# One-instruction modulation sums, bias and scale by section, the sums spread over merges, output projection and feed-forward, and other feed-forward pieces, in a two-layer DiT block on one core

## The chip, the cores and the metric

One core of a Trainium2 chip runs the whole kernel in one launch. The metric is device time in microseconds (us); lower is better. The times of before are three runs, and one more execution was profiled.

## What is computed

Two layers of a hybrid block on 512 latent tokens `x` and 256 context tokens `ctx`, width 1024, in float32. Cut to what matters here:

```python
def adaln(cond, w_mod, b_mod):
    return jnp.split(jax.nn.silu(cond) @ w_mod + b_mod, N_MOD, axis=-1)
...
        sh1, sc1, gt1, sh2, sc2, gt2 = [m[:, None, :] for m in adaln(c, w_mod[l], b_mod[l])]
        csh1, csc1, cgt1, csh2, csc2, cgt2 = adaln(c_ctx, w_mod[l], b_mod[l])
        h = modulate(rms_norm(x, norm1[l]), sh1, sc1)
        a_b, a_c, a_x, q, k, v, u, sv, g = project(h, w_in[l], q_gain[l], k_gain[l])
...
        x = x + gt1 * merge_branches(...)
        x = x + gt2 * swiglu(modulate(rms_norm(x, norm2[l]), sh2, sc2), w_ff1[l], w_ff3[l], w_ff2[l])
```

The context tokens go through the same weights with their own modulation `c_ctx`; in the second layer only their keys and values are needed. `merge_branches` is `(g_a * y_a + g_b * y_b + g_c * y_c) @ w_o`, with three sigmoid gates, each a projection of 1024 columns.

Each layer has six modulation vectors ("sections" 0 to 5: shift, scale and gate of the first half, shift, scale and gate of the second), each a product of a 1024-vector with a 1024x1024 matrix.

## The kernel before, in words

Activations lie transposed: channels in the 128 partitions, 8 blocks of them, tokens along the row (0 to 511 latent, 512 to 767 context). Every float32 operand of a large product is split in a high and a low part; a product is three matmuls, high x high, high x low, low x high (`mm`, L233 to L241, the matmuls at L240). Weights come by `load_piece` (L219 to L227): SP issues the load into `ws` (five buffers), ACT casts to `wh`, POOL or DVE subtracts to get `wl` (both by `split`, L229 to L231). All loads, of weights and of the modulation matrices, stand in one queue, SP's, which issues in order.

The stages of a layer: first norm (`norm`, `norm_stats` L349 to L372: squares on ACT, added to `nacc` by DVE at L358, a column sum on PE at L361 into `pst`, `ms` at L363, its power on POOL, `RR` at L368, transposed to `pRB`; then `norm_apply` L374 to L386 writes `ny` and the split arena tiles `A`), projections, attention, then the merges (L809 to L851). A merge j computes three gates of 768 columns: PE into banks, ACT's tanh at L815 into a `gate` buffer (two for the gates a and c of a width), DVE multiplies the branch into it at L821 and adds the parts at L830 and L836; ACT and POOL split the result `z`. The output projection (`wo_j`, L860 to L875) and the second norm by halves (`norm_half`) follow. In layer 0 the feed-forward takes pairs of columns by seven products in place of eight (`pair_product`, L310 to L346; `ff_pair`, L936 to L978; a pair has two of them, for `w_ff1` and `w_ff3`); the first pair is computed plainly (`first_pair`). The results `u`, split again by `keep_u`, go into `ff2_j` (L993 to L1007), piece by piece: layer 0's 22 column blocks come in the pieces of L980, and after each piece the second matrix of those blocks is added to X, eight outputs j. In the last piece `lagged` (L423 to L437) does outputs 0 to 3 in full, then 4 to 7 for the x columns, then 4 to 7 for the context columns, with the next layer's norm of x between them.

The modulation is done on DVE, from rows: one 128-row block of the transposed matrix is multiplied with the condition, which lies in all partitions (`sbc`), and summed along the row. `mod_block` (L152 to L171) does a block of a section: two loads of 128x512 (`wm`, six buffers, L156), and for each condition two multiply-and-sum instructions (L162, each followed by a read of the accumulator), one that adds both halves and the bias (L165) and in three sections a scaling (L169 or L171). The blocks of the first norm are called where it is. The other 80 come from a generator, `bg_all`: 32 blocks of layer 0 with two conditions, 16 of layer 1 with two, 32 of layer 1 with one, which makes 128 pairs of block and condition; `pump` draws from it after merges, output-projection columns, and feed-forward steps. `bg_stage` (L175 to L179) can hold a block's load back: POOL copies one column of a tile into the new `wm` buffer (L178), so that the load waits for that tile. Before, that tile is the last branch b from the merges to the end of the output projection and none later.

The program is written in one order, but the Tile framework schedules it with a model of the engines: what stands in which queue is decided there, by what an instruction waits for and not only by where it was written.

Of the kernel before, what the change touches and what calls it, by code (L numbers as in the profile page):

```python
# [9 lines left out]
F32 = mybir.dt.float32  # L10
# [21 lines left out]
NX = 6  # L32
# [5 lines left out]
def dit_block(ctx: ExitStack, tc: tile.TileContext, xT, conds, vecs, ident_in, rope_c, rope_s,  # L38
# [57 lines left out]
    def f(t):  # L96
        return t.bitcast(F32)
# [54 lines left out]
    def mod_block(l, sec, b, cs, stage):  # L152
        parts = []
        for hh in range(2):
            t = stage()
            nc.sync.dma_start(t, w_modT[l, sec * KD + b][:, hh * 512:(hh + 1) * 512])  # L156
            parts.append(t)
        for c in cs:
            acc = sm.tile([P, 2], F32, tag="macc", name="macc", bufs=4)
            for hh in range(2):  # L160
                junk = wp.tile([P, 512], F32, tag="junk", name="junk", bufs=1)
                nc.vector.scalar_tensor_tensor(junk, parts[hh], 1.0, sbc[:, c, hh * 512:(hh + 1) * 512],  # L162
                                               op0=ALU.mult, op1=ALU.mult, accum_out=acc[:, hh:hh + 1])
            m = MOD[l][:, sec, b, c:c + 1]
            nc.vector.scalar_tensor_tensor(m, acc[:, 0:1], vcol(l, V_BM + sec * KD + b), acc[:, 1:2],  # L165
                                           op0=ALU.add, op1=ALU.add)
            if sec in (1, 4):
                g, v = (G1, V_N1) if sec == 1 else (G2, V_N2)
                nc.vector.tensor_scalar(g[l][:, b, c:c + 1], m, 1.0, vcol(l, v + b), op0=ALU.add, op1=ALU.mult)  # L169
            elif sec == 2:  # L170
                nc.vector.tensor_scalar(GT1[l][:, b, c:c + 1], m, 0.5, None, op0=ALU.mult)  # L171

    gate_mods = [None]

# [6 lines left out]
    def wm_stage():  # L181
        return wp.tile([P, 512], F32, tag="wm", name="wm", bufs=6)

    def bg_all():
        for sec in (2, 4, 3, 5):
            for b in range(KD):
                mod_block(0, sec, b, (0, 1), bg_stage)
                yield
        for sec in (1, 0):
            for b in range(KD):  # L190
                mod_block(1, sec, b, (0, 1), bg_stage)
                yield
        for sec in (2, 4, 3, 5):
            for b in range(KD):
                mod_block(1, sec, b, (0,), bg_stage)
                yield
# [269 lines left out]
    n_stage = [0]  # L466

    def first_stage():

        t = wm_stage()  # L470
        n_stage[0] += 1
        if n_stage[0] <= 6:
            nc.gpsimd.tensor_copy(t[:, 0:1], X[NX][:, 0:1])
        return t

    for l in range(2):
# [79 lines left out]
        if l == 0:  # L556
            six = [wide[0][:, 0:512], wide[0][:, 512:], wide[1][:, 0:512], wide[1][:, 512:], pst("D"), pst("D")]
            RB = norm_stats(X, *XS)
            for k in range(KD):
                for sec in (1, 0):  # L560
                    mod_block(0, sec, k, (0,), first_stage)
# [147 lines left out]
        if l == 0:  # L709
            def ctx_mods():  # L710
                for k in range(KD):
                    for sec in (1, 0):
                        mod_block(0, sec, k, (1,), wm_stage)
                    yield
# [118 lines left out]
        def merge_b(j, tag):  # L833
# [6 lines left out]
            if not last:  # L840
                pump(3)
# [18 lines left out]
        def wo_j(j, sg):  # L860
# [14 lines left out]
            pump()  # L875
# [6 lines left out]

        gate_mods[0] = None


        def plain(f0, f1, U):
            for n in range(f0, f1):
# [14 lines left out]
                pump()  # L902

        def keep_u(su, U):
            hi, lo = two("u", W)
            split(su, hi, lo)
            U.append((hi, lo))

        def first_pair(U):
# [15 lines left out]
            for n in range(2):  # L925
# [8 lines left out]
                keep_u(su[n], U)  # L934

        def ff_pair(m, U):  # L936
# [142 lines left out]
```

## Time and profile before

| | |
|---|---|
| median of three runs | 1995.39 us (1991.87 to 1998.12) |
| the profiled execution | 1999.56 us, its span 1997.8 us |
| granted TensorE clock | 0.979 |
| PE busy | 1888.2 us (95%), 10150 matmuls |
| DVE busy | 1252.6 us (63%) |
| ACT, POOL busy | 746.9 us (37%), 836.1 us (42%) |
| modulation loads | 224 of 256 KB, 4.1 us each from issue to landing |

PE is TensorE, DVE VectorE, ACT ScalarE, POOL GpSimd, SP the engine that issues loads. A row of a group gives line, engine, operation, tiles (out<-in, without buffer numbers), shapes, count, busy us and mean ns, and after a second bar the idle time before them and what ended it. A row of waits reads "engine line <- what it waited for: us in all, times, longest". A row of a time line gives start, length, engine and line, and in brackets an idle time just before. Where DVE_READ_ACCUMULATOR stands, it belongs to the instruction ahead of it.

### The profile page before, as it was taken

What the parts mean: (1) busy time and instruction counts of PE and PEld (TensorE: products, weight loads), DVE (VectorE), ACT (ScalarE), POOL (GpSimd) and SP (SyncE); (2) the same over time, 40 slices, a digit from 0 to 9 for tenths busy, and PEclk for the clock granted to TensorE, in tenths of its full rate; (3) what the DMA queues carried; (4) which work ended last, traced back from release to release, by engine and by line L of the source; (5) the groups of instructions that cost most, each with busy time, mean ns of one, the idle gap of its engine ahead of it and who ended that gap; (6) DMA issues with size and microseconds to landing.
All of it is one profiled execution on the core that took longest, in us unless ns stands there. A gap on an engine that the chain in (4) does not pass through costs nothing.

```text
span 1997.8 us, 28465 instructions
## 1 busy us (share of the span) xinstructions
PE 1888.2 (95%) x10150; PEld 1661.1 (83%) x10150; DVE 1252.6 (63%) x2454; ACT 746.9 (37%) x1459; POOL 836.1 (42%) x720
## 2 busy tenths in 40 slices
PE   5789999989799899999999997999999999999999
PEld 4578998878679799999999996787888888888887
DVE  7987776999999974655667556648633362322322
ACT  4346766212112642423232235447533353313121
POOL 5577744645432332415142236754333243413231
PEclk9899999999989999999999998999999999999999
DMA  8833211644569222212122214410233244332311
GB/s 288 275 116 99 67 32 30 209 164 143 190 218 337 88 70 63 85 48 80 59 75 68 64 62 143 157 43 6 80 103 93 97 145 144 100 101 90 109 38 65
DMA packets 123871, 221.96 MB, mean 111 GB/s; under 512 B 14160, under 2 KB 22096, under 8 KB 123728
## 3 DMA queue, kind: packets, MB, share of 16 engines
q1 hardware_dynamic: 121664, 216.99, 33.5%
q10 hardware_dynamic: 2064, 3.15, 0.5%
q8 instruction: 80, 1.31, 0.3%
q14 instruction: 63, 0.52, 0.1%
HBM read 212.22 MB, written 5.24 MB: 109 GB/s over the span
## 4 chain that ended last, share of the span: by engine, by line
PE 59%; DVE 4%; issue 2%; ACT 1%; POOL 1%; DMA 0%; ACTq 0%; DVEq 0%; POOLq 0%; SPq 0%
PE wide L240 22%; PE pD L240 18%; PE wide L317 7%; PE pD L317 7%; PE pF L240 1%; PE pO L777 1%; PE pPT L771 1%; PE wide L745 1%; DVE ptl L774 0%; DVE nm L749 0%; DVE nacc L358 0%; DVE xr L998 0%; POOL wl L231 0%; DVE qq L549 0%; DVE qb L537 0%
## 5 line engine op out<-in xcount | busy, mean ns | idle before, releaser
L231 POOL TENSOR_TENSOR wl<-ws,wh 128x512 fp32r<-128x512 f32 (+2 forms) x338 | 458.8, 1368 | 550.1 <-ACT wh L230 392.2
L240 PE MATMUL wide<-A,wh 128*128 128x512 f32 (+2 forms) x1728 | 479.3, 373 | 43.6 <-ACT gate L815 19.0
L240 PEld LDWEIGHTS wide<-A,wh 128*128 128x128 f32 x1728 | 307.8, 195 | 103.1 <-ACT gate L815 20.6
L230 ACT CAST wh<-ws 128x512 fp32r<-128x512 f32 (+2 forms) x536 | 302.3, 606 | 79.3 <-DVE junk L162 30.9
L240 PE MATMUL wide<-A,wl 128*128 128x512 f32 (+2 forms) x864 | 291.4, 369 | 3.5 <-POOL wl L231 3.5
L231 DVE TENSOR_TENSOR wl<-ws,wh 128x512 fp32r<-128x512 f32 (+1 forms) x198 | 173.7, 877 | 142.0 <-ACT wh L230 78.0
L162 DVE SCALAR_TENSOR_TENSOR junk<-wm,fixed 128x512 f32<-128x512 f32 x320 | 253.7, 804 | 7.0 <-DMA wm<-in_w_modT 4.2
L240 PE MATMUL pD<-A,wh 128*128 128x512 f32 (+1 forms) x784 | 237.2, 383 | 6.9 <-DVE acv L624 2.1
L240 PEld LDWEIGHTS wide<-A,wl 128*128 128x128 f32 x864 | 156.2, 195 | 29.2 <-POOL wl L231 4.5
L240 PEld LDWEIGHTS pD<-A,wh 128*128 128x128 f32 x784 | 146.4, 191 | 35.9 <-issue 2.4
L240 PE MATMUL pD<-A,wl 128*128 128x512 f32 (+1 forms) x392 | 148.9, 381 | 1.7 <-POOL wl L231 1.7
L240 PE MATMUL wide<-u,wh 128*128 128x512 f32 (+1 forms) x608 | 149.7, 351 | 0.3 <-DVE xr L998 0.3
L240 PE MATMUL pD<-u,wh 128*128 128x512 f32 (+1 forms) x448 | 115.9, 357 | 1.9 <-POOL u L231 1.1
L240 PEld LDWEIGHTS wide<-u,wh 128*128 128x128 f32 x608 | 99.5, 188 | 16.2 <-DVE xr L998 0.5
L754 POOL TENSOR_SCALAR pp<-pp,nm 128x768 f32<-128x768 f32 (+1 forms) x80 | 67.1, 841 | 97.3 <-DVE nm L753 66.7
L231 POOL TENSOR_TENSOR u<-su,u 128x768 fp32r<-128x768 f32 (+1 forms) x44 | 72.7, 1661 | 80.3 <-ACT u L230 80.3
L998 DVE SCALAR_TENSOR_TENSOR xr<-wide,fixed,xr 128x512 f32<-128x512 f32 (+1 forms) x70 | 42.0, 634 | 101.3 <-PE wide L240 101.3
L230 ACT CAST u<-su 128x768 fp32r<-128x768 f32 (+1 forms) x44 | 32.0, 728 | 196.1 <-DVE su L896 93.7
L815 ACT ACTIVATE gate<-wide 128x512 f32<-128x512 f32 (+1 forms) x56 | 26.7, 516 | 180.2 <-PE wide L240 81.2
L240 PE MATMUL wide<-u,wl 128*128 128x512 f32 (+1 forms) x304 | 89.6, 351 | 0.0
L240 PEld LDWEIGHTS pD<-A,wl 128*128 128x128 f32 x392 | 74.7, 190 | 16.3 <-POOL wl L231 2.3
L240 PEld LDWEIGHTS pD<-u,wh 128*128 128x128 f32 x448 | 75.0, 188 | 14.8 <-POOL u L231 1.4
(245 smaller groups left out, 3783.0 us busy)
## 6 DMA issues: line engine op xcount, KB each, us to landing
ws<-in_w SPq DMA_DIRECT2D x248, 256.0 KB, 2.7
wm<-in_w_modT SPq DMA_DIRECT2D x224, 256.0 KB, 4.1
ws<-in_w_in SPq DMA_DIRECT2D x184, 256.0 KB, 3.0
ws<-in_w_o SPq DMA_DIRECT2D x48, 256.0 KB, 5.3
ws<-in_w_abc SPq DMA_DIRECT2D x32, 256.0 KB, 2.7
ws<-in_w_six SPq DMA_DIRECT2D x16, 192.0 KB, 4.7
xr<-in_xT SPq DMA_DIRECT2D x8, 384.0 KB, 7.0
ws<-in_w SPq DMA_DIRECT2D x16, 192.0 KB, 2.7
```

What stands on the lines that cost most here:

```text
L162: nc.vector.scalar_tensor_tensor(junk, parts[hh], 1.0, sbc[:, c, hh * 512:(hh + 1) * 512], op0=ALU.mult, op1=ALU.mult, accum_out=acc[:, hh ...
L230: nc.scalar.copy(hi, src)
L231: (lo_eng or nc.gpsimd).tensor_tensor(lo, src, f(hi), op=ALU.subtract)
L240: nc.tensor.matmul(d[:, :b - a], lhsT=ww, rhs=aa[:, a:b], start=kk == 0 and i == 0, stop=kk == n - 1 and i == 2)
L317: nc.tensor.matmul(D, lhsT=x[:, kk * P:(kk + 1) * P], rhs=a, start=kk == 0 and i == 0, stop=kk == 3 and i == 2)
L745: nc.tensor.matmul(D[:, a - k0:b - k0], lhsT=q[:, c * P - q0:(c + 1) * P - q0], rhs=kt[:, a:b], start=i == 0, stop=i == 1)
L754: nc.gpsimd.tensor_scalar(pt[:, :nk], pt[:, :nk], nm[:, 3:4], 0.0, op0=ALU.mult, op1=ALU.add)
L771: nc.tensor.transpose(TD[:, (2 * j + cc) * P:(2 * j + cc + 1) * P], pts[cc][:, kc:kc + P], ident)
L777: nc.tensor.matmul(o[:, 0:256], lhsT=v3[:, kt, :], rhs=pp[:, j * 256:(j + 1) * 256], start=gi == 0 and j == 0 and i == 0, stop=gi == len(k ...
L815: nc.scalar.activation(g_[:, a:e], D, AF.Tanh, scale=0.5)
L998: nc.vector.scalar_tensor_tensor(X[j][:, a:b], D, MOD[l][:, 5, j, c:c + 1], X[j][:, a:b], op0=ALU.mult, op1=ALU.add)
```

## The change

The sums: `mod_sums` takes a block with one load of 128x1024 (three buffers of the same memory) and one multiply-and-sum per condition, which adds straight into the modulation vector; the last condition writes its products over the loaded tile. `mod_rest` adds the bias and scales once per section, over its 8 blocks and all its conditions (in the first norm of x still by block).

The places: the holding tile is now the merge's own `z` (three blocks a merge), the output column `Xn[j]` of the first four output-projection columns (two blocks each), and in layer 0's feed-forward the last `u` or the last `X[j]`, with one block per product and per odd j. So layer 0's 32 blocks stand in merges and output projection, and layer 1's 48 blocks (64 pairs) in layer 0's feed-forward. The loads of the first norm are no longer held behind X. The feed-forward pieces of layer 0 start with two column blocks instead of ending with two.

```diff
-    def mod_block(l, sec, b, cs, stage):
...
+    def mod_sums(l, sec, b, cs, t):
+
+        nc.sync.dma_start(t, w_modT[l, sec * KD + b])
         for c in cs:
...
+            o = t if c == cs[-1] else wp.tile([P, 1024], F32, tag="junk", name="junk", bufs=1)
+            nc.vector.scalar_tensor_tensor(o, t, 1.0, sbc[:, c, :], op0=ALU.mult, op1=ALU.mult,
+                                           accum_out=MOD[l][:, sec, b, c:c + 1])
+
+    def mod_rest(l, sec, b0, n, c0, nc_):
+
+        m = MOD[l][:, sec, b0:b0 + n, c0:c0 + nc_]
+
+        def col(off):
+            return vcol(l, off + b0, n)[:, :, None].to_broadcast([P, n, nc_])
+        nc.vector.tensor_tensor(m, m, col(V_BM + sec * KD), op=ALU.add)
+        if sec in (1, 4):
+            g, v = (G1, V_N1) if sec == 1 else (G2, V_N2)
+            nc.vector.scalar_tensor_tensor(g[l][:, b0:b0 + n, c0:c0 + nc_], m, 1.0, col(v), op0=ALU.add, op1=ALU.mult)
+        elif sec == 2:
+            nc.vector.tensor_scalar(GT1[l][:, b0:b0 + n, c0:c0 + nc_], m, 0.5, None, op0=ALU.mult)
...
+    def wm_stage():
+        return wp.tile([P, 1024], F32, tag="wm", name="wm", bufs=3)
...
+                    mod_sums(l, sec, b, cs, bg_stage())
+                    if b == KD - 1:
+                        mod_rest(l, sec, 0, KD, 0, len(cs))
+                    yield
...
             if not last:
+                gate_mods[0] = f(hi[:, W - 1:W])
                 pump(3)
...
-            pump()
+            if j < 4 and not last:
+                gate_mods[0] = Xn[j][:, W - 1:W]
+                pump(2)
...
-        gate_mods[0] = None
...
             split(su, hi, lo)
             U.append((hi, lo))
+            gate_mods[0] = f(hi[:, W - 1:W])
...
-        parts = [(0, 8), (8, 15), (15, 22)] if last else [(0, 4), (4, 8), (8, 12), (12, 16), (16, 20), (20, 22)]
+            pump()
+
+        parts = [(0, 8), (8, 15), (15, 22)] if last else [(0, 2), (2, 6), (6, 10), (10, 14), (14, 18), (18, 22)]
...
+                if not last and j % 2:
+                    gate_mods[0] = X[j][:, W - 1:W]
+                    pump()
```

DVE's queue in a merge before. L162 are sums, L165 and L171 their additions and scalings, L821, L830 and L836 the merge's own multiplications and adds.

```order
L165 SCALAR_TENSOR_TENSOR fixed<-macc,fixed 128x1
L821 SCALAR_TENSOR_TENSOR gate<-gate,pD 128x512
L162 SCALAR_TENSOR_TENSOR junk,macc<-wm,fixed 128x512
L171 TENSOR_SCALAR fixed<-fixed 128x1
L821 SCALAR_TENSOR_TENSOR gate<-gate,pD 128x256
L162 SCALAR_TENSOR_TENSOR junk,macc<-wm,fixed 128x512
L836 TENSOR_TENSOR gate<-gate 128x768
L165 SCALAR_TENSOR_TENSOR fixed<-macc,fixed 128x1
L162 SCALAR_TENSOR_TENSOR junk,macc<-wm,fixed 128x512
L171 TENSOR_SCALAR fixed<-fixed 128x1
```

The sums fill every gap between the merge's own instructions. The same place after (here with buffer numbers; L156 is a sum, L809 a multiplication, L818 and L824 the adds):

```order
L809 SCALAR_TENSOR_TENSOR gate_3846<-gate_3846,pD_3915 128x512
L809 SCALAR_TENSOR_TENSOR gate_3846<-gate_3846,pD_3916 128x256
L824 TENSOR_TENSOR gate_3683<-gate_3683,gate_3846 128x768
L156 SCALAR_TENSOR_TENSOR junk_3950,fixed_74<-wm_3947,fixed_74 128x1024
L156 SCALAR_TENSOR_TENSOR wm_3947,fixed_74<-wm_3947,fixed_74 128x1024
L156 SCALAR_TENSOR_TENSOR junk_3956,fixed_74<-wm_3953,fixed_74 128x1024
L156 SCALAR_TENSOR_TENSOR wm_3953,fixed_74<-wm_3953,fixed_74 128x1024
L156 SCALAR_TENSOR_TENSOR junk_3962,fixed_74<-wm_3959,fixed_74 128x1024
L156 SCALAR_TENSOR_TENSOR wm_3959,fixed_74<-wm_3959,fixed_74 128x1024
L809 SCALAR_TENSOR_TENSOR gate_3965<-gate_3965,pD_4097 128x512
```

A merge's six sums now stand together behind its last add (L824, which gives `z`), ahead of the next merge's first multiplication.

DVE's queue where layer 0 ends, before: the last added squares, the statistics of x (128x4) and of the context (128x2), the spread `RR` of both, and the first modulated values.

```order
L358 TENSOR_TENSOR nacc<-nacc,nsq 128x512
L358 TENSOR_TENSOR nacc<-nacc,nsq 128x256
L363 TENSOR_SCALAR ms<-pst 128x4
L363 TENSOR_SCALAR ms<-pst 128x2
L368 COPY RR<-rr 128x512
L368 COPY RR<-rr 128x256
L380 SCALAR_TENSOR_TENSOR ny<-xr,fixed,pRB 128x512 x4
```

And after, where L990 is an output of the second matrix and L156 a sum:

```order
L352 TENSOR_TENSOR nacc<-nacc,nsq 128x512
L352 TENSOR_TENSOR nacc<-nacc,nsq 128x256
L990 SCALAR_TENSOR_TENSOR xr<-pD,fixed,xr 128x256
L352 TENSOR_TENSOR nacc<-nacc,nsq 128x256
L357 TENSOR_SCALAR ms<-pst 128x4
L352 TENSOR_TENSOR nacc<-nacc,nsq 128x256 x2
L357 TENSOR_SCALAR ms<-pst 128x2
L362 COPY RR<-rr 128x512
L156 SCALAR_TENSOR_TENSOR wm,fixed<-wm,fixed 128x1024
L362 COPY RR<-rr 128x256
L374 SCALAR_TENSOR_TENSOR ny<-xr,fixed,pRB 128x512 x4
L156 SCALAR_TENSOR_TENSOR wm,fixed<-wm,fixed 128x1024
```

The statistics of x stand before the last squares of the context, and one sum has come between the two `RR`, another behind the first four `ny`.

SP's queue in layer 0's feed-forward before: weights of the products (L257) and of the second matrix (L224).

```order
L224 DMA ws<-in_w_o 128x512 x2
L224 DMA ws<-in_w 128x512 x8
L257 DMA ws<-in_w 128x512 x8
L224 DMA ws<-in_w 128x512 x8
L257 DMA ws<-in_w 128x512 x16
L224 DMA ws<-in_w 128x512 x8
L257 DMA ws<-in_w 128x512 x16
```

And after, where L153 is a modulation load that waits for a copy on POOL, L251 a product's weights and L218 the second matrix's:

```order
L153 DMA wm<-in_w_modT 128x1024 x2
L218 DMA ws<-in_w 128x512 x7
L251 DMA ws<-in_w 128x512
L153 DMA wm<-in_w_modT 128x1024
L251 DMA ws<-in_w 128x512 x2
L153 DMA wm<-in_w_modT 128x1024
L251 DMA ws<-in_w 128x512 x3
L153 DMA wm<-in_w_modT 128x1024
L251 DMA ws<-in_w 128x512
L153 DMA wm<-in_w_modT 128x1024 x3
L251 DMA ws<-in_w 128x512 x9
L153 DMA wm<-in_w_modT 128x1024 x2
```

In such a round eight modulation loads now stand at five places ahead of weight loads. The copies that they wait for are new in POOL's queue there, up to four in a row, ahead of the subtractions for `wl`; before, POOL had there only these subtractions and the feed-forward's own multiplications and subtractions.

More of the change, by code (lines that the diff above doesn't have):

```diff
@@ L31 @@
 CS = (SEQ, NT)
-NX = 6
 HT = NT // 2
@@ L150, in dit_block @@
     GT1 = [keep(KD, 2) for l in range(2)]
-    def mod_block(l, sec, b, cs, stage):
[L153 to L157, printed above, removed]
-        for c in cs:
[L159 to L171, printed above, removed]
+    def mod_sums(l, sec, b, cs, t):
+        nc.sync.dma_start(t, w_modT[l, sec * KD + b])
+        for c in cs:
+            o = t if c == cs[-1] else wp.tile([P, 1024], F32, tag="junk", name="junk", bufs=1)
[11 more added lines that the diff above has]
+            nc.vector.tensor_scalar(GT1[l][:, b0:b0 + n, c0:c0 + nc_], m, 0.5, None, op0=ALU.mult)
     gate_mods = [None]
+    def wm_stage():
+        return wp.tile([P, 1024], F32, tag="wm", name="wm", bufs=3)
     def bg_stage():
@@ L179, in bg_stage @@
         return t
-    def wm_stage():
-        return wp.tile([P, 512], F32, tag="wm", name="wm", bufs=6)
     def bg_all():
[L185 to L196, printed above, removed]
+        for l, secs, cs in ((0, (2, 4, 3, 5), (0, 1)), (1, (1, 0), (0, 1)), (1, (2, 4, 3, 5), (0,))):
+            for sec in secs:
+                for b in range(KD):
+                    mod_sums(l, sec, b, cs, bg_stage())
+                    if b == KD - 1:
+                        mod_rest(l, sec, 0, KD, 0, len(cs))
+                    yield
     bg = bg_all()
@@ L465, in dit_block @@
     nc.scalar.activation(sbc[:, 0, :], sbc[:, 0, :], AF.Silu)
[L466 to L474, printed above, removed]
     for l in range(2):
@@ L560, in dit_block @@
                 for sec in (1, 0):
-                    mod_block(0, sec, k, (0,), first_stage)
+                    mod_sums(0, sec, k, (0,), wm_stage())
+                    mod_rest(0, sec, k, 1, 0, 1)
                 norm_apply(X, RB, G1[0], MOD[0][:, 0], k, *XS, h[k])
@@ L712, in ctx_mods @@
                     for sec in (1, 0):
-                        mod_block(0, sec, k, (1,), wm_stage)
+                        mod_sums(0, sec, k, (1,), wm_stage())
+                        if k == KD - 1:
+                            mod_rest(0, sec, 0, KD, 1, 1)
                     yield
@@ L901, in plain @@
                 keep_u(su, U)
-                pump()
         def keep_u(su, U):
@@ L976, in ff_pair @@
             pair_product(pair_weights(w_13[l, 0, 2 * m:2 * m + 2]), four("tp"), silu11, silu12, silu21, silu22)
+            pump()
             tmp3 = four("tp")
             pair_product(pair_weights(w_13[l, 1, 2 * m:2 * m + 2]), tmp3, mul11, mul12, mul21, mul22)
-        parts = [(0, 8), (8, 15), (15, 22)] if last else [(0, 4), (4, 8), (8, 12), (12, 16), (16, 20), (20, 22)]
+            pump()
+        parts = [(0, 8), (8, 15), (15, 22)] if last else [(0, 2), (2, 6), (6, 10), (10, 14), (14, 18), (18, 22)]
         for pi, (f0, f1) in enumerate(parts):
@@ L1000, in ff2_j @@
                 gemm(w, U, sg, ev)
+                if not last and j % 2:
+                    gate_mods[0] = X[j][:, W - 1:W]
+                    pump()
                 if f1 == NFF:
```

1 line of the change is left out of this document (removed).

## The prediction

> **What bounds the kernel now.** I read the page first: the span, the engines' busy shares and the slices of time.
>
> ```profile
> span 1997.8 us, 28465 instructions
> PE 1888.2 (95%) x10150; PEld 1661.1 (83%) x10150; DVE 1252.6 (63%) x2454; ACT 746.9 (37%) x1459; POOL 836.1 (42%) x720
> PE   5789999989799899999999997999999999999999
> DVE  7987776999999974655667556648633362322322
> ```
>
> Each slice is 50 us. PE is full nearly everywhere; where its row falls below 9 the time can shrink, since the change adds and removes no matmul. The low slices are the first two, those between 350 and 750 us, and the one at 1200. (The one at 1350 to 1450 is layer 1's attention, which the change doesn't touch.) In the second group DVE's row stands at 9. So I asked for the stages by windows. The columns are length, then busy time of PE, PEld, DVE, ACT, POOL (instructions), the granted PE clock, DMA share and GB/s.
>
> ```profile
> core 0: us, PE busy (x) PEld busy (x) DVE busy (x) ACT busy (x) POOL busy (x), PEclk, DMA share, GB/s
> 0.00:50.00 50.00, 26.16 (x99) 20.66 (x100) 37.81 (x91) 20.25 (x33) 25.60 (x38) 1.00 0.88 289
> 50.00:100.00 50.00, 37.19 (x148) 28.03 (x147) 47.17 (x110) 17.98 (x36) 26.60 (x20) 0.86 0.85 274
> 348.70:663.00 314.30, 291.50 (x1621) 255.57 (x1620) 308.12 (x800) 69.88 (x135) 142.93 (x136) 0.96 0.62 210
> 663.00:735.00 72.00, 62.92 (x323) 57.97 (x322) 60.22 (x113) 40.55 (x88) 27.23 (x19) 0.93 0.17 52
> 750.00:1150.00 400.00, 399.79 (x2306) 379.99 (x2305) 241.34 (x377) 117.62 (x211) 123.53 (x88) 1.00 0.22 67
> 785.60:844.00 58.40, 58.40 (x339) 58.38 (x338) 42.23 (x65) 21.39 (x39) 18.19 (x13) 1.00 0.26 77
> 1200.00:1225.00 25.00, 14.12 (x51) 11.03 (x51) 19.18 (x31) 14.20 (x26) 14.75 (x16) 0.66 0.48 168
> 1450.00:1600.00 150.00, 149.69 (x661) 123.62 (x660) 48.36 (x75) 48.51 (x89) 48.40 (x36) 1.00 0.32 101
> ```
>
> The stage from 348.7 to 663 us is layer 0's merges and most of its output projection. DVE is busy 98% of it, PE idles 314.30 - 291.50 = 22.8 us, and at a mean clock of 0.96 some 0.04 x 291.5 = 12 us more go to a lower clock. Layer 1's merges and output projection (1450 to 1600) are the same work without modulation: 0.3 us idle in 150, clock 1.00. The feed-forward of layer 0 (750 to 1150) has PE idle 0.2 us in 400 while DVE is at 60%. So the modulation work sits in the one stage where it hurts, and none of it where DVE has room.
>
> The waits of that stage, for PE and then for ACT, and DVE's two costliest groups there:
>
> ```profile
> PE wide L240 <- ACT gate L815: 19.0, 5, 6.2
> ```
> ```profile
> ACT gate L815 <- DVE junk L162: 38.8, 6, 11.3
> ACT gate L815 <- issue: 28.5, 2, 15.1
> ACT gate L815 <- PE wide L240: 22.1, 3, 9.7
> ```
> ```profile
> L162 DVE SCALAR_TENSOR_TENSOR junk<-wm,fixed 128x512 f32<-128x512 f32 x256 | 195.0, 774 | 4.3 <-DMA wm<-in_w_modT 4.2
> L165 DVE SCALAR_TENSOR_TENSOR fixed<-macc,fixed 128x1 f32<-128x1 f32 x127 | 66.9, 527 | 3.6
> ```
>
> PE's stalls have one name: a bank that ACT's gate activation hasn't emptied. ACT can't write the gate because a gate buffer is still held by the multiplications and adds (L821 to L836) that stand in DVE's queue behind modulation sums. These two groups are 262 of DVE's 308 us; what else DVE does there is under 50 us.
>
> **The sums as one instruction.** The price of one (block, condition) pair, undisturbed, is in DVE's time line:
>
> ```profile
> 597.63 0.68 DVE L162 SCALAR_TENSOR_TENSOR junk<-wm,fixed 128x512 f32<-128x512 f32 x1
> 598.24 0.08 DVE L162 DVE_READ_ACCUMULATOR junk<-wm,fixed 128x1 f32 x1
> 598.31 0.68 DVE L162 SCALAR_TENSOR_TENSOR junk<-wm,fixed 128x512 f32<-128x512 f32 x1
> ...
> 599.04 0.22 DVE L165 SCALAR_TENSOR_TENSOR fixed<-macc,fixed 128x1 f32<-128x1 f32 x1
> 599.17 0.69 DVE L162 SCALAR_TENSOR_TENSOR junk<-wm,fixed 128x512 f32<-128x512 f32 x1
> ```
>
> From one pair's first sum to the next pair's, 599.17 - 597.63 = 1.54 us; in the whole stage (195.0 + 66.9) / 128 = 2.05 us, since the sums take 774 ns instead of 680 and the one-column additions 527 instead of 220. A 128x1024 sum isn't in the trace. The second half of a 512-wide one starts 0.68 us after the first (597.63 and 598.31), so two are an upper bound of 1.36. Below, the row
>
> ```profile
> L836 DVE TENSOR_TENSOR gate<-gate 128x768 f32<-128x768 f32 x8 | 7.6, 951 | 0.0
> ```
>
> gives (0.95 - 0.68) / 256 columns, hence 0.68 + 2 x 0.27 = 1.22 us. I take 1.22, plus up to 0.3 where POOL works beside it (527 - 220 ns is what such an instruction lost): 1.2 to 1.5 us. A pair's addition and scaling fall to 1/16 or 1/8 of one instruction: nothing. [...]
>
> **Merges and output projection.** The old generator gave everything out here, 128 pairs; the new one gives 24 blocks to the merges and 8 to the output projection, 64 sums. DVE's load is 308 - 262 + 64 x (1.2 to 1.5) = 123 to 142 us of some 285: half. In the order a merge's six sums (7 to 9 us) stand behind its last add and ahead of the next merge's multiplications, which come one gate pair later on PE; two gate buffers and three pairs of banks cover that. What was lost, 22.8 + 12 = 35 us, should go down to about layer 1's level; I keep 4 us for places where six sums and a late load (512 KB each, three in a row) still meet the multiplications: **-31**, between -20 and -34.
>
> **First norm.** Sixteen pairs before the first x projections, each 0.3 us shorter, and no load held behind X: ACT waits there on the additions.
>
> ```profile
> ACT A L382 <- DVE fixed L165: 8.6, 4, 3.3
> ACT ny L385 <- DVE fixed L165: 5.4, 3, 2.7
> ```
>
> 14 us at most could go, but DMA is at 0.88 and loads what the sums need; a 512 KB piece also lands 256 KB / 289 GB/s = 0.9 us later than a half. **-3**, between -8 and +2.
>
> **Between output projection and feed-forward (663 to 735).** PE idles 9 us there behind the two half norms. Sixteen sums of the output projection now stand ahead of them in place of the old ones: two standing before a step of the chain cost 3 us, a lighter queue before it gives as much back. **+1**, between -3 and +4.
>
> **Feed-forward of layer 0.** It gets 64 sums, 77 to 96 us, in the 466 us from 735 to the last matmul at 1201.5: DVE from 60% to 77 to 81%. Mostly hidden. Two places aren't sure. In the first pair behind the short part (0,2), eight sums stand within about one product. A product takes 58.40 / 4 = 14.6 us with 42.23 / 4 = 10.6 of DVE; with 8 x 1.5 that is 22.6, so 8 us too much if nothing slips, and I take 3. And POOL's and SP's queues hold copies and loads that wait for X[j] or u, ahead of weight splits:
>
> ```profile
> L231 POOL TENSOR_TENSOR wl<-ws,wh 128x512 fp32r<-128x512 f32 x31 | 42.6, 1383 | 124.7 <-ACT wh L230 68.7 <-DVE fw L269 28.2 <-DMA ws<-in_w 27.8
> L231 POOL TENSOR_TENSOR u<-su,u 128x768 fp32r<-128x768 f32 x18 | 36.5, 2048 | 0.0
> ```
>
> One late split costs its 1.4 us; at the five turns from the second matrix to the next products I take 0.6 each, 3 us. **+6**, between 0 and +15.
>
> **Into layer 1.** PE's and DVE's time lines at the end of layer 0:
>
> ```profile
> 1201.03 0.40 PE L240 MATMUL wide<-u,wh 128*128 128x256 f32 x2
> 1201.27 0.28 PE L240 MATMUL wide<-u,wl 128*128 128x256 f32 x1
> 1209.02 1.87 PE L361 MATMUL pst<-fixed,nacc 128*128 128x1 f32 x8 [7.47 <-DVE nacc L358]
> ...
> 1216.27 0.79 PE L240 MATMUL wide<-A,wh 128*128 128x512 f32 x1 [2.35 <-ACT A L230]
> ```
> ```profile
> 1204.39 4.91 DVE L358 TENSOR_TENSOR nacc<-nacc,nsq 128x512 f32<-128x512 f32 x8
> 1210.93 0.16 DVE L363 TENSOR_SCALAR ms<-pst 128x4 f32<-128x4 f32 x1 [1.62 <-PE pst L361]
> ```
>
> After PE's last matmul (1201.55) the statistics follow 9.4 us later and the next matmul 14.7 us later. The last part had two pieces, so PE handed over results faster than DVE added squares. With four, PE's context half of the last four outputs (4 x 12 matmuls of 256 columns; two take 1201.27 - 1201.03 = 0.24 us, so 5.8 us) runs behind the x half, and DVE keeps up: the statistics should come 1 to 2 us after the last matmul, about 8 us sooner. Of that one sum between the copies of RR and the first multiplication costs 1.2 if its load is there: **-7**, between -11 (the low clock, 0.66 in these 25 us, shortens too) and +3 (the load is gated on the last X and POOL's copy, and holds DVE).
>
> **The sum** is -31 - 3 + 1 + 6 - 7 = -34 us. The profiled execution took 1999.56 us, 4.2 above the median of the three timed runs, 1995.39; -34 on the median gives 1961.
>
> **The rivals.**
> *The gates don't wait for DVE.* The waits of ACT for PE (22.1 us) and for issue (28.5) speak for it: then half of PE's loss in the merges stays, -31 becomes -14, and the time is 1978. Against it: DVE at 98%, and the same gates cost layer 1 nothing. 0.10.
> *The feed-forward gives half back.* A long DVE instruction and POOL keep each other waiting: u on POOL took 2048 ns, a split of two thirds its width 1383, and sums beside POOL were 774 for 680. If three sums of 1.2 us stand in POOL's way at the end of every pair of products, u is 3.7 us late at five parts, and with the dense place in full (8) the cost is 26 instead of 6: 1981. [...] Against it: POOL is busy only 31% of this stage. 0.13.
> *Slower: the gated loads starve PE.* SP issues in order, and in the feed-forward 48 modulation loads now stand among the weight loads, each behind a POOL copy that waits for a u or an X. If PE loses G at each, the change costs 48 G against the other terms' -40: it decides from G = 0.83 us; at 1 us the time is 1995 - 40 + 48 = 2003. For it: no such wait exists in this stage before, and POOL has up to four such copies in a row. Against it: PE's slack (0.2 us idle in 400) and five weight buffers. 0.07.
> *More than forecast.* First norm -8, into layer 1 -11, nothing lost in the feed-forward, -34 in the merges: 1995 - 53 + 1 = 1943. 0.06.
>
> **How the numbers follow.** The forecast, 1961, has 0.64. With 1978 and 1981 the range goes from 1944 to 1985; it leaves out the slower rival, some of the best case, and a little of the tails. Two runs of this kernel can be told apart by about 0.3%, 6 us. Faster by more than that is below 1989: the forecast, both partial cases and the best one, less a tail, 0.88. Within it 0.05; slower 0.07.
>
> **What would show it.** In the changed kernel's profile: groups of 128x1024 sums at 1.2 to 1.5 us; DVE at about half in the merges and PE idle under 4 us there, clock near 1.00; no ACT gate waiting for a sum; DVE near 80% in the feed-forward with PE idle under 10 us; PE's gap before layer 1 near 7 us instead of 14.7. I would be wrong if a sum took 2 us, if PE waited for wl or u at every turn of the feed-forward, or if the merges still lost over 15 us with DVE half idle.

## The result and the profile after

The changed kernel takes 1974.16 us (median of four runs, 1973.0 to 1976.47), the kernel before 1996.41 (four runs beside it): a ratio of 0.9893, 95% interval 0.9874 to 0.9913, some 22 us faster. Its profiled execution has a span of 1973.4 us, 24.4 less than the one before. One run of the changed kernel's second measurement, at the end of the experiments, took 1996.09 us at a granted clock of 0.916, which widens the interval given there.

The page of the changed kernel, the lines that answer to those of before:

```profile
span 1973.4 us, 27588 instructions
PE 1879.8 (95%) x10150; PEld 1654.6 (84%) x10150; DVE 1164.6 (59%) x1936; ACT 747.8 (38%) x1459; POOL 859.9 (44%) x722
PE   5789999999999899999999998999999999999999
DVE  7877865535359887877676867549523362322222
```

DVE's row tells the change at a glance: its nines between 350 and 590 us have become threes and fives (a nine stays behind them), and the fours to sevens of the feed-forward (from 700 to 1150) have become sixes to eights. PE's row has lost its dips of the merges. Now the windows; the third and fourth have the ends that the rows of before had, moved by what the kernel is ahead there; the last two are PE's gap at the entry to layer 1 and layer 1's projections.

```profile
0.00:50.00 50.00, 25.36 (x99) 20.15 (x100) 36.44 (x68) 20.60 (x33) 25.04 (x32) 1.00 0.83 281
50.00:100.00 50.00, 37.03 (x162) 29.42 (x161) 43.95 (x65) 16.89 (x34) 31.76 (x20) 0.90 0.91 303
348.70:632.50 283.80, 282.29 (x1603) 247.64 (x1601) 149.90 (x232) 68.52 (x135) 118.93 (x100) 1.00 0.40 141
632.50:704.00 71.50, 62.77 (x324) 57.36 (x324) 55.53 (x108) 37.65 (x86) 30.80 (x25) 0.93 0.14 45
1183.00:1193.30 10.30, 3.29 (x18) 2.73 (x17) 9.06 (x19) 3.39 (x8) 6.42 (x8) 0.61 0.79 264
1193.30:1299.00 105.70, 105.54 (x514) 88.56 (x515) 62.29 (x84) 50.99 (x93) 81.54 (x61) 0.97 0.35 111
```

The stage of merges and output projection takes 283.8 us instead of 314.3. PE idles 1.5 us in it instead of 22.8, its clock is 1.00 instead of 0.96, and DVE is at 53%. The waits of PE, and the first of ACT's, in that window:

```profile
PE wide L234 <- DVE xr L861: 1.5, 1, 1.5
```
```profile
ACT gate L803 <- PE wide L234: 140.0, 19, 10.7
```

No gate waits for a sum any more: ACT now waits for PE, as it should where PE is the bound. A 128x1024 sum, minimum, median and maximum in ns:

```profile
L156 DVE SCALAR_TENSOR_TENSOR wm<-wm,fixed x112: 1207/1224/2301, 13.9 to 1193.6; 128x1024 f32<-128x1024 f32 x112
L156 DVE SCALAR_TENSOR_TENSOR junk<-wm,fixed x48: 1208/1218/2308, 358.7 to 855.6; 128x1024 f32<-128x1024 f32 x48
```

The medians, 1224 and 1218 ns, are the 1.22 us that was worked out from the 512-wide and the 768-wide row.

To see where the two profiles part I cut both at six events: the first score matmul of layer 0's attention, the last output of its output projection on DVE, the last matmul of its second matrix, layer 1's first matmul, layer 1's first score matmul, and the end. The lengths in us:

| stage | before | changed | difference |
|---|---|---|---|
| start to attention | 172.7 | 171.4 | -1.3 |
| attention, merges, output projection | 503.2 | 474.0 | -29.2 |
| second norm and feed-forward, layer 0 | 525.6 | 537.5 | +11.9 |
| gap of PE at the entry to layer 1 | 14.7 | 10.3 | -4.5 |
| layer 1's projections | 110.1 | 105.8 | -4.4 |
| the rest of layer 1 | 671.4 | 674.4 | +3.0 |

They sum to -24.4 (before rounding). The stage with the loss is the one that was meant to hide the work. In the feed-forward DVE's busy time went from 328 to 410 us (windows of these two stages):

```profile
675.90:1201.50 525.60, 515.76 (x2929) 488.77 (x2928) 327.94 (x532) 173.58 (x332) 165.12 (x119) 0.99 0.22 67
```
```profile
645.50:1183.00 537.50, 518.90 (x2928) 489.63 (x2928) 410.25 (x669) 177.18 (x337) 195.72 (x166) 0.99 0.34 114
```

In the last 479 us of this stage before, PE idled 2.3 us:

```profile
722.40:1201.50 479.10, 476.77 (x2742) 453.45 (x2740) 289.31 (x460) 146.12 (x269) 146.73 (x107) 1.00 0.23 71
```

In the changed kernel (692 to 1183 us) it has these waits there, 10.8 us in all:

```profile
PE wide L311 <- DVE xr L990: 3.4, 1, 3.4
PE pD L311 <- DVE wl L225: 2.4, 1, 2.4
PE pD L311 <- DVE tp L330: 2.2, 2, 1.1
PE wide L311 <- ACT wh L224: 1.1, 1, 1.1
PE wide L234 <- DVE xr L990: 0.9, 1, 0.9
PE wide L311 <- DVE wl L225: 0.8, 1, 0.8
```

The longest, 3.4 us, ends at 717.38. DVE's time line ahead of it:

```profile
711.95 1.13 DVE L990 SCALAR_TENSOR_TENSOR xr<-pD,fixed,xr 128x512 f32<-128x512 f32 x2
713.01 2.11 DVE L156 SCALAR_TENSOR_TENSOR wm<-wm,fixed 128x1024 f32<-128x1024 f32 x1
715.05 0.07 DVE L156 DVE_READ_ACCUMULATOR wm<-wm,fixed 128x1 f32 x1
715.05 1.21 DVE L156 SCALAR_TENSOR_TENSOR junk<-wm,fixed 128x1024 f32<-128x1024 f32 x1
...
716.20 1.13 DVE L990 SCALAR_TENSOR_TENSOR xr<-wide,fixed,xr 128x512 f32<-128x512 f32 x2
```

The short first piece has handed its outputs to DVE; the last of them, which would empty a bank that the next product needs, stands behind two sums. The first of them took 2.11 us instead of 1.21; a weight split on POOL ran beside it:

```profile
712.74 1.29 POOL L225 TENSOR_TENSOR wl<-ws,wh 128x512 fp32r<-128x512 f32 x1 [1.27 <-ACT wh L224]
```

The second wait ends at 821.01, and here the sum itself waits for its load:

```profile
818.07 1.23 DVE L156 SCALAR_TENSOR_TENSOR junk<-wm,fixed 128x1024 f32<-128x1024 f32 x1 [1.13 <-DMA wm<-in_w_modT]
819.22 0.08 DVE L156 DVE_READ_ACCUMULATOR junk<-wm,fixed 128x1 f32 x1
819.22 1.74 DVE L225 TENSOR_TENSOR wl<-fw,wh 128x512 fp32r<-128x512 f32 x1
```
```profile
813.93 1.11 POOL L180 COPY wm<-xr 128x1 f32<-128x1 f32 x2 [8.44 <-DVE xr L990]
```
```profile
805.51 9.88 SPq L153 DMA_DIRECT2D wm<-in_w_modT  x3
```

POOL's copy waited 8.4 us for an output of X, SP's queue spent 9.9 us on three of these loads, and the weight split that PE needs stood behind the sum (and took 1.74 us where its like took 0.68 just before). Two causes are on offer, then: the DVE time of the sums, or the queues held for them. One thing speaks against the queues already: at the three later turns (899, 992 and 1085 us) SP spends 8.7 us on such loads each time, and behind 825 us PE has no wait but the two at `tp`. All its other waits lie where each block still brings two sums, of which the last `junk` starts at 855.6.

The entry to layer 1, PE and then DVE:

```profile
1182.73 0.28 PE L234 MATMUL pD<-u,wl 128*128 128x256 f32 x1
1184.50 1.15 PE L355 MATMUL pst<-fixed,nacc 128*128 128x1 f32 x8 [1.49 <-DVE nacc L352]
...
1193.27 0.80 PE L234 MATMUL wide<-A,wh 128*128 128x512 f32 x1 [2.30 <-ACT A L224]
```
```profile
1186.12 0.15 DVE L357 TENSOR_SCALAR ms<-pst 128x4 f32<-128x4 f32 x1
1189.31 0.43 DVE L362 COPY RR<-rr 128x512 f32<-128x512 f32 x1
1189.65 1.22 DVE L156 SCALAR_TENSOR_TENSOR wm<-wm,fixed 128x1024 f32<-128x1024 f32 x1
...
1191.01 2.72 DVE L374 SCALAR_TENSOR_TENSOR ny<-xr,fixed,pRB 128x512 f32<-128x512 f32 x4
```

The statistics of x come 3.1 us after the last matmul (1186.12 - 1183.01) instead of 9.4. The sum between the copies of RR stands there as the order had it, and its load was there.

### The profile page after: what moved, and what is told of

It reads as the page before. It is cut to its first block, busy times and chain, and to the rows that moved or that the text cites. A ratio compares the mean times of both kernels' runs of the same rounds, so it can differ in the third digit from the quotient of the medians.

```text
span 1973.4 us, 27588 instructions
## 1 busy us (share of the span) xinstructions
PE 1879.8 (95%) x10150; PEld 1654.6 (84%) x10150; DVE 1164.6 (59%) x1936; ACT 747.8 (38%) x1459; POOL 859.9 (44%) x722
## 4 chain that ended last, share of the span: by engine, by line
PE 73%; DVE 14%; issue 4%; ACT 3%; DMA 3%; POOL 2%; ACTq 0%; SPq 0%; DVEq 0%; POOLq 0%
PE wide L234 33%; PE pD L234 21%; PE pD L311 5%; PE wide L311 5%; PE pF L234 3%; DMA wm<-in_w_modT 2%; DVE wm L156 2%; PE pO L765 2%; DVE wl L225 2%; PE pPT L759 1%; PE wide L733 1%; DVE junk L156 1%; DVE nm L737 1%; DVE nacc L352 1%; DVE ptl L762 1%
## 5 line engine op out<-in xcount | busy, mean ns | idle before, releaser
L225 POOL TENSOR_TENSOR wl<-ws,wh 128x512 fp32r<-128x512 f32 (+2 forms) x338 | 484.4, 1445 | 462.5 <-ACT wh L224 376.0
L234 PE MATMUL wide<-A,wh 128*128 128x512 f32 (+2 forms) x1728 | 469.3, 367 | 17.4 <-ACT A L224 8.2
L234 PEld LDWEIGHTS wide<-A,wh 128*128 128x128 f32 x1728 | 302.8, 192 | 72.7 <-ACT A L224 10.2
L224 ACT CAST wh<-ws 128x512 fp32r<-128x512 f32 (+2 forms) x536 | 302.2, 607 | 65.4 <-issue 17.5
L225 DVE TENSOR_TENSOR wl<-ws,wh 128x512 fp32r<-128x512 f32 (+1 forms) x198 | 168.4, 851 | 131.5 <-ACT wh L224 121.5
L156 DVE SCALAR_TENSOR_TENSOR wm<-wm,fixed 128x1024 f32<-128x1024 f32 x112 | 152.1, 1361 | 49.4 <-DMA wm<-in_w_modT 47.5
L156 DVE SCALAR_TENSOR_TENSOR junk<-wm,fixed 128x1024 f32<-128x1024 f32 x48 | 68.2, 1420 | 54.3 <-DMA wm<-in_w_modT 47.2
L809 DVE SCALAR_TENSOR_TENSOR gate<-gate,pD 128x512 f32<-128x512 f32 (+1 forms) x45 | 25.6, 596 | 122.4 <-PE pD L234 99.8
L224 ACT CAST wh<-fw 128x512 fp32r<-128x512 f32 x80 | 48.5, 615 | 121.8 <-DVE fw L263 106.3
L224 ACT CAST u<-su 128x768 fp32r<-128x768 f32 (+1 forms) x44 | 31.7, 728 | 165.7 <-DVE su L885 93.9
```

What stands on the lines that cost most here:

```text
L156: nc.vector.scalar_tensor_tensor(o, t, 1.0, sbc[:, c, :], op0=ALU.mult, op1=ALU.mult, accum_out=MOD[l][:, sec, b, c:c + 1])
L224: nc.scalar.copy(hi, src)
L225: (lo_eng or nc.gpsimd).tensor_tensor(lo, src, f(hi), op=ALU.subtract)
L234: nc.tensor.matmul(d[:, :b - a], lhsT=ww, rhs=aa[:, a:b], start=kk == 0 and i == 0, stop=kk == n - 1 and i == 2)
L809: nc.vector.scalar_tensor_tensor(g_[:, a:e], g_[:, a:e], 1.0, D, op0=ALU.add, op1=ALU.mult)
```

## The experiments

**One part at a time.** First the form alone, on the kernel before:

```diff
-                mod_block(0, sec, b, (0, 1), bg_stage)
+                    mod_sums(l, sec, b, cs, bg_stage())
+                    if b == KD - 1:
+                        mod_rest(l, sec, 0, KD, 0, len(cs))
...
-        return wp.tile([P, 512], F32, tag="wm", name="wm", bufs=6)
+        return wp.tile([P, 1024], F32, tag="wm", name="wm", bufs=3)
```

> The kernel before with the new form of the sums alone (one 128x1024 sum, bias and scale by section); places, holds and feed-forward pieces as before. All 128 pairs are still drawn into the merges, some 20 sums a merge. If the form carried the gain of the merges: DVE there falls from 308 us by 128 x (2.05 - 1.4) = 83 us, PE loses little, and the time is 1996 - 25 = 1971 or so. If the place carried it (my theory): 20 sums a merge of 1.4 us are 28 us beside some 5 us of the merge's own work in 36 us, DVE stays near 80 to 90% there and gates still wait for sums; about half of the gain, 1996 - 14 = 1982.

Measured: 1987.43 us against 1993.8 of before, ratio 0.9964 (0.9953 to 0.9976). The merges' window of that kernel, and PE's longest wait in it:

```profile
348.70:657.00 308.30, 290.59 (x1622) 254.17 (x1621) 262.07 (x370) 72.41 (x142) 156.91 (x107) 0.97 0.63 212
```
```profile
PE wide L235 <- DVE gate L819: 15.9, 5, 7.2
```

DVE is down to 85%, and PE still idles 17.7 us, 15.9 of them at these gates. The form shortens the work but leaves the crowd: 7 us of the 22, where I expected 14. DVE's work fell by 46 us instead of 83, since the sums took 1.50 and 1.74 us in the mean in that crowd.

Then the places and holds alone, with the old form and the old pieces:

```diff
             if not last:
+                gate_mods[0] = f(hi[:, W - 1:W])
                 pump(3)
...
-            pump()
+            if j < 4 and not last:
+                gate_mods[0] = Xn[j][:, W - 1:W]
+                pump(2)
...
-        gate_mods[0] = None
...
+                if not last and j % 2:
+                    gate_mods[0] = X[j][:, W - 1:W]
+                    pump()
```

> The kernel before with the new places and holds alone; the sums as two 128x512 halves with their small additions, the pieces of the feed-forward as before. If the place carries the merges' gain: -29 us there as in the changed kernel, but the feed-forward gets 64 pairs of 2.05 in place of 1.4 us, 131 us on DVE in 466 (60% to 88%), and loses some 20 to 25 us; no gain at the entry to layer 1, where two held blocks now stand: 1996 - 29 + 22 = 1989. If the feed-forward hides the longer form as well: 1970.

Measured: 1985.11 us, ratio 0.9951 (0.9929 to 0.9973). The merges are as good as in the changed kernel, and the gap of PE at the entry to layer 1 grows:

```profile
348.70:634.50 285.80, 284.43 (x1615) 249.80 (x1614) 179.85 (x445) 69.79 (x138) 116.32 (x134) 1.00 0.41 140
```
```profile
1178.30:1197.90 19.60, 3.99 (x17) 3.42 (x16) 18.45 (x44) 5.01 (x11) 8.85 (x11) 0.57 0.81 290
```

From attention to the last output this kernel takes 477.6 us: 25.6 of the merges' 29.2 us come from the place. The feed-forward took 530.9, only 5.3 more than before, where I expected 22, though DVE was busy there for 417 us, more than the changed kernel's 410; the gap at its end is 19.6 us instead of 14.7 and the projections behind it take 111.7.

Then the changed kernel with the old order of pieces:

```diff
-        parts = [(0, 8), (8, 15), (15, 22)] if last else [(0, 2), (2, 6), (6, 10), (10, 14), (14, 18), (18, 22)]
+        parts = [(0, 8), (8, 15), (15, 22)] if last else [(0, 4), (4, 8), (8, 12), (12, 16), (16, 20), (20, 22)]
```

> The changed kernel with the old order of feed-forward pieces, two column blocks last. If the entry to layer 1 owes its gain to the four-block last piece: that gain goes (about 8 us), and the crowd of sums behind the first short piece (3.4 us of stall) goes too: 1974 + 8 - 3 = 1979. If the gain there came from elsewhere (sums moved, holds): no change, 1974, or a little faster.

Measured: 1979.54 us, ratio 0.9922 (0.9898 to 0.9945).

```profile
1175.70:1195.90 20.20, 3.97 (x16) 3.43 (x16) 16.82 (x29) 4.90 (x11) 8.94 (x7) 0.51 0.73 273
```

With a last piece of two blocks and held sums in it the gap is 20.2 us; with four blocks 10.3. But the feed-forward with the old pieces takes 529.4 us, 8.1 less than with the new ones. The order of pieces gives 10 us at the end and takes 8 at the beginning. (In the profiles the two kernels are 2.0 us apart, in the medians 5.)

**What the feed-forward pays for.** The changed kernel without layer 1's modulation (its sums, loads and holds left out):

```diff
+                    if l == 1:
+                        if b == 0:
+                            nc.vector.tensor_copy(MOD[1][:, sec, :, 0:len(cs)], MOD[0][:, sec, :, 0:len(cs)])
...
+                        yield
+                        continue
                     mod_sums(l, sec, b, cs, bg_stage())
```

> The changed kernel without layer 1's modulation sums: it leaves out their 48 loads, holds and 64 sums (layer 1 then takes layer 0's sums with its own biases). This prices what the moved work costs where it now stands. If the feed-forward's 12 us of lost time come from these sums and holds: PE loses nothing there, and two sums less stand at the entry to layer 1 (2 to 3 us): 1974 - 12 - 2 = 1960. If the loss there is of another source (the pieces, the clock): 1972.

Measured: 1968.23 us, ratio 0.9866 (0.9847 to 0.9886). The feed-forward takes 525.4 us, as before, and the gap is 6.6. So the moved work costs all of the 11.9 us and 3.7 of the gap. In total only 6 us came out of that. In the profile layer 1's projections took 112.2 us instead of 105.8 (PE waits for a `wl` of POOL there), and the start to attention, whose queues the scheduler ordered otherwise here, 176.0 instead of 171.4.

To tell work from holds, the sums cut to 16 columns, with loads, copies and places kept:

```diff
-    def mod_sums(l, sec, b, cs, t):
+    def mod_sums(l, sec, b, cs, t, cut=False):
...
-            nc.vector.scalar_tensor_tensor(o, t, 1.0, sbc[:, c, :], op0=ALU.mult, op1=ALU.mult,
+            n = 16 if cut else 1024
+            nc.vector.scalar_tensor_tensor(o[:, :n], t[:, :n], 1.0, sbc[:, c, :n], op0=ALU.mult, op1=ALU.mult,
...
-                    mod_sums(l, sec, b, cs, bg_stage())
+                    mod_sums(l, sec, b, cs, bg_stage(), l == 1)
```

> The changed kernel with layer 1's sums cut to 16 of their 1024 columns (it leaves out the rest of these sums): the 48 loads, their copies on POOL and their places in SP's queue stay, DVE's work for them nearly goes. The feed-forward of layer 0 took 525.6 us before, 537.5 in the changed kernel, 525.4 without sums, loads and holds. If DVE's work is what costs (my theory): 526 to 528 us here, and about 1965 in all. If the held loads in SP's and POOL's queues cost: 535 or more, 1972.

Measured: 1965.38 us, ratio 0.986 (0.9842 to 0.9878).

```profile
646.60:1170.00 523.40, 513.67 (x2936) 486.83 (x2936) 346.87 (x674) 179.21 (x341) 187.07 (x168) 1.00 0.35 118
```

The feed-forward takes 523.4 us, less even than before, with every load and hold in place. From 690 us on SP still waits 255 us for POOL's copies (274 in the changed kernel), POOL's copies 80 us for X (118), and DVE as long as ever for modulation loads (55 us in both). So held queues and late loads cost PE nothing by themselves; the long sums on DVE are needed for the loss (its busy time falls from 410 to 347 us). Short sums also take away what POOL and DVE lengthen each other by (a sum of 2.11 us beside POOL's split above, where its like took 1.21); the run doesn't separate the two.

**Can it be had for less?** The short piece as the fifth:

```diff
-        parts = [(0, 8), (8, 15), (15, 22)] if last else [(0, 2), (2, 6), (6, 10), (10, 14), (14, 18), (18, 22)]
+        parts = [(0, 8), (8, 15), (15, 22)] if last else [(0, 4), (4, 8), (8, 12), (12, 16), (16, 18), (18, 22)]
```

> The changed kernel with the two-block piece as the fifth of six instead of the first, the last piece still of four. If the crowd of sums behind the short first piece costs most of the feed-forward's 12 us, as the run with the old pieces suggests (3.8 us lost there): 7 to 8 us less in the feed-forward with the entry to layer 1 as good as in the changed kernel, 1974 - 7 = 1967. If the loss comes with any short piece, wherever it stands: 1974.

Measured: 1975.09 us, ratio 0.9901 (0.9886 to 0.9915). The feed-forward went to 529.8 us, 7.7 less, as expected, and the gap stayed at 10.6. The total didn't follow: layer 1's projections took 111.8 us instead of 105.7, with PE waiting in them:

```profile
PE pD L234 <- POOL wl L225: 3.7, 2, 2.1
```

Without the hold on X in the feed-forward:

```diff
                 if not last and j % 2:
-                    gate_mods[0] = X[j][:, W - 1:W]
                     pump()
```

> The changed kernel without the hold on X[j] in the feed-forward: blocks drawn there wait for the last u alone. In the changed kernel POOL waits 118 us in all at copies from X, SP up to 9.9 us at a stretch and DVE 55 us for modulation loads. If these held queues cause PE's stalls: 4 to 8 us less, 1968. If DVE's mere load does: no change, 1974, or slower where the loads come earlier and the sums crowd.

Measured: 1971.58 us, ratio 0.9883 (0.9869 to 0.9898). POOL's waits at these copies fell from over 118 to 37 us in all; the feed-forward took 533.9 us (3.7 less than the changed kernel), the gap 12.7. In the total that can't be told apart from the changed kernel's 0.9893 (0.9874 to 0.9913). In the stage it can, which repeats well (537.5 and 537.3 us, below): with every sum at its full length PE's longest wait from 692 us on is 1.1 us instead of 3.4. So while the sums are long, the holds help to decide in front of what a sum lands.

The short piece late and no block drawn in the last piece:

```diff
-                pump()
+                pump(n + 1)
...
-                if not last and j % 2:
+                if not last and f1 != NFF and (j % 2 or j == 2):
```

> The two-block piece as the fifth, and no block drawn in the last piece: six blocks more in the earlier ones (one more at the second block of the first pair, one more in each second-matrix pass but the last, at output 2). The sums between the norm's steps at the entry to layer 1 go. The gap of PE there was 10.3 us with them and 6.6 in the run without layer 1's sums: 3 to 4 us less than the kernel with the short piece late, 1964 if that one makes 1967. If the two sums there were hidden, the same as that one.

Measured: 1970.2 us, ratio 0.9878 (0.9862 to 0.9894).

```profile
1180.40:1187.40 7.00, 1.73 (x9) 1.65 (x9) 5.33 (x10) 1.82 (x4) 2.27 (x3) 0.76 0.44 136
```

The gap went to 7.0 us, as without layer 1's sums, and the projections behind it took 107.0; the feed-forward, with six blocks more before its end, took 532.9.

Then one weight subtraction in three on DVE before layer 1's merges, on the kernel with the short piece late:

```diff
-        lo_engs[0] = [nc.gpsimd]
+        lo_engs[0] = [nc.gpsimd, nc.gpsimd, nc.vector] if last else [nc.gpsimd]
```

> The kernel with the short piece late (1975), and one in three of the weight subtractions before layer 1's merges on DVE instead of POOL. If what the shorter feed-forward saved was given back to POOL (PE waits 3.7 us for wl in layer 1's projections there, and a low clock follows): that stretch of 111.9 us goes to 105, and the time to 1969. If the stretch is bound by something else, such as the chain of the norm: 1975.

Measured: 1975.29 us, ratio 0.9899 (0.9884 to 0.9914). POOL's work in layer 1's projections fell from 79.6 to 64.9 us, and the stretch only from 111.8 to 110.2; PE still waits 3.0 us for a `wl`. So it isn't POOL's load as a whole.

The traces show what the long cases share. The step that turns queries and keys by position fills a tile `sw` by transfers, and POOL multiplies it (L531 here) once they have landed. In the five experiments in which PE waits for `wl`, and in no other kernel here, the first three of these multiplications stand in POOL's queue with no weight split between them. Each of PE's waits for `wl` there is for a split right behind two or three of them in a row. The kernel with the short piece late, and then the changed kernel at the same place:

```profile
1222.54 1.68 POOL L531 TENSOR_TENSOR sw<-sw,ropeS 128x512 f32<-128x512 f32 x1
1227.05 1.28 POOL L531 TENSOR_TENSOR sw<-sw,ropeS 128x512 f32<-128x512 f32 x1 [2.83 <-DMA sw<-qq]
1228.28 4.66 POOL L225 TENSOR_TENSOR wl<-ws,wh 128x512 fp32r<-128x512 f32 x3
```
```profile
1227.73 1.44 POOL L225 TENSOR_TENSOR wl<-ws,wh 128x512 fp32r<-128x512 f32 x1 [1.04 <-ACT wh L224]
1229.14 1.73 POOL L531 TENSOR_TENSOR sw<-sw,ropeS 128x512 f32<-128x512 f32 x1
```

No run changes this order alone, so it is read from the traces and not tested. All of these edits together (short piece late, no block in the last piece, no hold on X, a third on DVE):

> Short piece late, no block in the last piece, no hold on X, and one subtraction in three on DVE before layer 1's merges. If the four gains add: feed-forward 528 us, gap at the entry to layer 1 of 7 us, the stretch behind it 105 us: 1962. If each only moves the wait to the next engine in the chain: 1970, as the best of the single ones.

Measured: 1972.31 us, ratio 0.9886 (0.9871 to 0.9901). The gap was 6.1 us and the projections 107.0, but the feed-forward took 538.6: the gains don't add. The changed kernel once more, beside these two:

> The changed kernel once more, beside the two variants on one chip: 1974. Its stages tell how far one profile repeats: every theory expects the six stages within 1 us of the first profile; where they aren't, that much of a difference between kernels means nothing.

Measured: 1977.22 us, ratio 0.9921 (0.9893 to 0.995). Its profile's stages are 172.6, 474.4, 537.3, 11.3, 106.1 and 674.3 us, all within 1.3 of the first where 1 was expected, and the waits of PE in the feed-forward stand at the same matmuls (3.4, 1.1, 2.6, 1.1 and 1.1 us). The start to attention stands in the same order in ten of the profiles (changed kernel included) and took 170.6 to 173.3 us in them. So differences of 4 to 8 us between stages of two kernels belong to their orders and not to chance, while 3 us between two totals, or in the first stage, can be either. Last, the kernel with the free end once more:

> The kernel with the short piece late and no block in the last piece once more, to see whether it beats the changed kernel: if its first 1970 was its level, the ratio to the kernel before is again 0.988 and lies under the changed kernel's 0.989 to 0.992; if that was the chip's spread, 0.990 or more.

Measured: 1969.64 us, ratio 0.9865 (0.9849 to 0.9881). In two measurements each it has 0.9878 and 0.9865 against the changed kernel's 0.9893 and 0.9921: some 5 us better by the medians, with intervals that touch in three of the four pairings, so that isn't certain.

## Why the prediction was right, and where its sum was off

The direction, the stage and the mechanism were right; the gain was 22 us where the sum said 34. As a time, 1974 lies nearer to the two partial rivals (1978 and 1981) than to 1961. Of the signs that were named, two failed: PE idles 18.6 us in the stage of the feed-forward (10.8 from 692 us on), not under 10, and its gap is 10.3 us, not near 7.

*Merges and output projection, -31:* -29.2 in a stage that begins a little earlier, and -30.5 in the window itself. In the window PE's idle time fell by 21.3 us and its busy time by 9.2 (291.50 to 282.29): 1.5 us of idle time are left, and the lower clock, taken as 12 us, was some 3 too dear. The 4 us kept back covered just these two, though they were meant for late loads; that is luck. The places carry the gain (25.6 of 29.2 with the old form), the form alone 9; with the old places the form is worth 7 us on the total, and under the new places and old pieces some 6 (0.9951 to 0.9922).

*First norm, -3:* -1.3 in one profile, -0.1 in the repeat, within the spread of that stage. The DMA share in the first 100 us is 0.83 and 0.91, about as before, but DVE waits only 5.4 us for modulation loads from 10 to 100 us; why the shorter sums gained nothing wasn't tried.

*Between output projection and feed-forward, +1:* 0. The window took 71.5 us against 72.0; the half norms were as late, behind the same wait for A (2.4 us, 2.3 before).

*Feed-forward, +6:* +11.9, within the 0 to 15 given but double the value: 8.8 us of it are idle time of PE, 3.1 its longer busy time. This is the step that failed in size. "Mostly hidden" held for the totals (DVE at 76%) and not at the places: a dense place costs what stands ahead of the one DVE instruction that PE needs next. I gave the crowd behind the short piece 3 us; its one long stall cost 3.4 and the low-clock stretch behind it (3.40 us at 0.50) an estimated 1.7, and the waits up to 824.5 us come to 8.5. That beginning is what the place of the short piece moves (7.7 us). The five turns I priced at 0.6 each for POOL's and SP's holds; of the four behind that one, only the turn at 821 us cost anything, and there a weight split stood behind a sum that itself came 1.1 us late for its load. With the sums cut short and the holds kept, all waits of PE from 690 us to the end of the stage are gone but the two of 1.1 us at `tp`; with the sums long and the hold on X gone, the two longest are gone too. So it takes both: a long sum, and something that puts it in front of what PE needs.

*Into layer 1, -7:* -4.5 in the gap and -4.4 behind it. The first is less than expected because the context's squares and one sum stood between, and POOL took the power of the statistics only at 1187.59, behind two weight splits; the run without layer 1's sums has a gap of 6.6. The second wasn't in the sum and is luck: without it the profile would have gained 20 us. Layer 1's projections take 105 to 106 us in some orders, 107 in others and 110 to 112 in others again. In all of the long ones PE waits for one instruction late in a queue (2.1 us for `acv` on DVE before, 3.0 to 4.3 us for `wl` on POOL in five of the experiments). Before, the clock is 0.50 from 1283.92 to 1287.33, right behind that wait; in the five the mean clock of the stretch is 0.95 to 0.97, where it is 0.97 in the changed kernel.

*Not in the sum:* +3.0 in the rest of layer 1, whose code is untouched. In the experiments it took 671.5 to 674.7 us, with and without layer 1's sums; what sets it wasn't tried.

Of the rivals, the one with gates that don't wait for DVE fell with the first window: ACT's gates wait for PE alone. The feed-forward that gives half back was nearer than the forecast in its place (+12 of its +26) though its mechanism was only in part the one named: POOL and DVE do lengthen each other, which is some 0.9 us of the longest stall (a sum of 2.11 us beside POOL's split against 1.21) and 1.1 of the second (a split of 1.74 on DVE against 0.68, while POOL's split beside it, at 818.17, took 2.24 against 1.29). But no `u` was late: its subtraction on POOL took 2016 ns in the mean in this stage, 2028 before, and PE waits for DVE itself. Nor did the rows it was argued from show a wait: 2048 ns for 768 columns and 1383 for 512 are the same 2.7 ns a column. The slower rival's queues were really held (9.9 us on SP) and starved nobody.

What stays open: why the scheduler orders an untouched stage one way or the other, and whether a split between the three `sw` multiplications alone would bring the long projections down to 105 us. Taking load from POOL didn't.

## What to carry to other kernels

When one engine's background work fills a stage in which the bound engine waits for it, move the work to a stage with room; in that stage it was worth nearly three times as much as making the work itself cheaper (25.6 us against 9.1; on the totals, after what the other stages lost, 10 against 7). Price the new place not by its mean load but by what a background instruction can stand in front of: in the changed kernel PE paid for sums of 1.2 us, or 2.1 beside POOL, where its next input stood behind them in DVE's queue (3.4 us at 717.38, 2.4 at 821.01), while 417 us of DVE work in shorter instructions and another order of pieces cost 5.3 us where 410 cost 11.9 here. And with a scheduler that reorders all queues, follow a saving past its own stage to the end before counting it: in one experiment 7.7 us were saved in the feed-forward and 6 lost to another order within the next 110 us; in another 8.1 were saved there and none lost in that stretch.

## What was not expected of the hardware

Holding SP's issue queue at gated loads, 48 of them among weight loads, cost PE nothing as long as the sums were short: SP waited 255 us for POOL's copies there, the stage took 523.4 us against 525.6 before, and from 690 us on no wait of PE was for a weight.

And behind some of PE's stalls of 2 to 4 us the granted clock was 0.50 for 3.4 us, so that such a stall cost more than its length. The 3.4 us stall that ends at 717.38 is followed by this:

```profile
717.70:721.10 3.40, 3.40 (x12) 3.40 (x11) 3.40 (x6) 0.00 (x0) 0.27 (x1) 0.50 0.52 154
```

Three matmuls of 384 columns take 0.96 us there (717.93 to 718.89), and 0.52 right behind it (721.65 to 722.17).

It isn't so each time. Behind the changed kernel's stall of 2.4 us at 821.01 the clock is 1.00; in the repeat, where the order is the same and the stall 2.6 us, half clock follows it:

```profile
822.20:825.60 3.40, 3.40 (x12) 3.40 (x12) 3.40 (x7) 0.00 (x0) 0.00 (x0) 0.50 0.35 133
```
